# Feed-forward h turned in 32x32 blocks on VectorE and carried between partitions by transfers

## The chip, the cores and the metric

The kernel runs on one core of a Trainium2 chip. Its engines work side by side, each in the order of its own instruction list: TensorE (PE) multiplies matrices, VectorE (DVE) and ScalarE (ACT) work on tiles, GpSimd (POOL) does a little, and SyncE (SP) issues the transfers. Tiles lie in SBUF, 128 partitions wide; TensorE writes into PSUM, which has eight banks. The metric is the device time of one execution in microseconds (us), the median of several runs.

## The reference

Two layers of a streaming encoder on x of 256 x 1024 in float32. Each layer is a feed-forward half step, a mixer (attention over frames and over a memory of 256 entries) and a second feed-forward half step. The change concerns the four feed-forward parts alone:

```python
def swiglu(h, w_gate, w_up, w_down):
    return (jax.nn.silu(h @ w_gate) * (h @ w_up)) @ w_down

for i in range(DEPTH):                                   # DEPTH = 2
    h = rmsnorm(x, ffn1_norm[i])
    x = x + 0.5 * swiglu(h, ffn1_w_gate[i], ffn1_w_up[i], ffn1_w_down[i])
    ...                                                  # the mixer
    h = rmsnorm(x, ffn2_norm[i])
    x = x + 0.5 * swiglu(h, ffn2_w_gate[i], ffn2_w_up[i], ffn2_w_down[i])
```

w_gate and w_up are 1024 x 2816, w_down is 2816 x 1024.

## The kernel before

**Exact products from two parts.** Every operand of a dense product is split into a rounded part and a remainder (hi and lo), and each tile of a product is three matmuls: hi x hi, lo x hi, hi x lo (`dense`, lines 382, 385, 388). The weights are split on the chip.

**The weight stream.** Weights come in 164 chunks of 1 MB, in the order of use. `loader` takes one of three `raw` buffers and issues the chunk's transfers on SP (line 269): for gate and up two of 512 KB, a pair, for down one of 1 MB. `split_hi` casts a chunk in four pieces on ScalarE (line 301, tile hi), `split_lo` subtracts in four pieces on VectorE (line 313, tile lo). There are four buffers of hi and lo. A `raw` buffer is free once lo's fourth piece is done, and only then can the load three chunks later be issued; a hi/lo buffer is free once TensorE has used the chunk.

**A feed-forward part (`ffn`).** The 2816 columns are taken in 11 groups of 256. The gate/up phase makes, for each group, gate and up side by side in one PSUM bank for each of two token blocks (tb 0 and 1; two chunks of weights, 48 matmuls of 512 columns). The down phase then multiplies h by w_down, one chunk of 256 rows for each group, into four banks. Between the two stands `evac`, once a group: for each token block ScalarE makes sil = silu(gate) (line 488) and VectorE multiplies by up (line 491, tile h, tokens on partitions). The down product needs h with its 256 columns on partitions. So TensorE turns it, four 128x128 blocks into one PSUM bank (line 395, tile htp); ScalarE casts that to ht's first part (line 506) and VectorE subtracts for its second (line 508). All 11 ht of a part are kept until the down phase uses them.

**What sets the order.** Nothing is scheduled on the chip: `Flow` (line 47) writes each engine's list beforehand. It keeps its own clock (a matmul 0.216 us, a hop between engines `HOP` 0.22, a 512-wide VectorE operation 0.60) and lets each thread write its next instruction when that clock says that the operands are there. hi and lo pieces are idle threads, placed when their engine is reckoned free within `SLACK` (0.4 us). Threads that are ready go ahead of idle ones. On the chip the lists run in this order, each instruction waiting on semaphores for what it really needs; an instruction that waits holds up all that stand behind it on its engine. In a group the reckoned order on VectorE is: lo's first and second piece of the chunk just freed, h of token block 1, lo's third piece, then (on TensorE) the turns, lo's fourth piece, and with that the next weight pair on SP.

**Transfers and semaphores.** The transfers of the program signal eight semaphores in turn. Before SP issues one, it waits until the transfer eight places earlier has landed.

**Buffers.** SBUF tiles of 4 KB a partition come from `g4` (12 slots), of 2 KB from `g2` (19 slots), PSUM banks from `banks` (8). A thread can wait for slots (`has(n)`).

Of the kernel before, what the change touches and what calls it, by code (L numbers as in the profile page):

```python
# [44 lines left out]


class Flow:
    """Orders the program: work of the vector, scalar and GpSimd engines is placed between the dense
    matrix products by an estimate of when its operands are there."""

    def __init__(self):
        self.now = 0.0
# [90 lines left out]
def kernel(  # L143
# [32 lines left out]
    def bank(name, shape=(P, 4, P)):  # L176
        return banks.take(list(shape), F32, name)

# [1 line left out]
    g1row = const.tile([16, P], F32, name="g1row")  # L180
    nc.sync.dma_start(out=g1row, in_=ffn1_norm.rearrange("l (k p) -> (l k) p", p=P))
    xs = [const.tile([P, D], F32, name=f"x{tb}") for tb in range(2)]
# [52 lines left out]
        nc.vector.tensor_scalar_mul(gcs[:, 3:4], gcol[:, GC_SUB:GC_SUB + 1], 1.0 - LAMBDA_INIT)  # L235
        flow.dve(0, 0.5)

# [1 line left out]
    class Chunk:  # L239
        def __init__(self, parts, mem=False):  # L240
            self.parts, self.mem = parts, mem
# [13 lines left out]
    def add_chunk(parts, uses=8, mem=False):  # L255
        c = Chunk(parts, mem)
        c.uses = uses
        c.index = len(chunks)
        chunks.append(c)
        return c  # L260
# [59 lines left out]
    def k2(t):  # L320
        return t.rearrange("p (k n) -> p k n", k=2)
# [7 lines left out]
    def rows2(w, r):  # L329
        return [(lambda raw: k2(raw), w[r * 256:(r + 1) * 256, :].rearrange("(k p) n -> p k n", p=P))]  # L330

    plan = {}
    WI = (((0, 256), (768, 256)), ((1536, 512),),
          ((256, 256), (1024, 256)), ((512, 256), (1280, 256)), ((2048, 256), (2304, 256)))
# [2 lines left out]
    def plan_ffn(l, nm, wg, wu, wd):  # L337
        gu = []
        for g in range(NG):
            ids = []  # L340
            for c in range(2):
                pieces = 2 if len(chunks) < 2 else 1
                a = cols4(wg[l], c, g * 256, 256, 0, pieces)
                b = cols4(wu[l], c, g * 256, 256, 256, pieces)
                ids.append(add_chunk([q for ab in zip(a, b) for q in ab]))
            gu.append(ids)
        plan[l, nm, "gu"] = gu
        dn = []
        for c in range(NG):
            dn.append(add_chunk(rows2(wd[l], c)))  # L350
            if (l, nm) == (0, 1) and c == NG - 4:
                plan["mem"] = add_chunk(
                    [(lambda raw: raw.rearrange("p (b d) -> p b d", b=2), mem[0].rearrange("(b p) d -> p b d", p=P))],
                    mem=True)
        plan[l, nm, "dn"] = dn
# [17 lines left out]
        plan_ffn(l, 2, ffn2_w_gate, ffn2_w_up, ffn2_w_down)  # L373

    def dense(ps, xh, xl, ready, c, need, sl, start, stop):
        """One K tile of a product: three passes over the parts of both operands."""
        flow.until(lambda: c.lot[need] is not None and ready() is not None)
        flow.at(ready())
        flow.at(c.lot[need])
        at[0] = max(at[0], c.index)  # L380
        wh, wl = sl(c.hi), sl(c.lo)
        nc.tensor.matmul(out=ps, lhsT=xh, rhs=wh, start=start, stop=False)  # L382
        flow.pe(T_MM)
        flow.step()
        nc.tensor.matmul(out=ps, lhsT=xh, rhs=wl, start=False, stop=False)  # L385
        flow.pe(T_MM)
        flow.step()
        nc.tensor.matmul(out=ps, lhsT=xl, rhs=wh, start=False, stop=stop)  # L388
        c.uses -= 1
        if c.uses == 0:  # L390
            hl_left[0] += 1
        return flow.pe(T_MM)

    def turn(dst, src, flipped=False):
        nc.tensor.transpose(out=dst, in_=src, identity=flip if flipped else ident)  # L395
        return flow.pe(T_TR)
# [5 lines left out]
        nc.gpsimd.tensor_tensor(out=dst, in0=v[:, :n], in1=nhalf[:, :n], op=ALU.pow)  # L402
        yield flow.pool(0.3 + 0.165 * n)

# [1 line left out]
    class Xt:  # L406
        def __init__(self):
            self.h = [xtp.tile([P, KT, P], F32R, tag=f"xh{tb}", name=f"xh{tb}") for tb in range(2)]
# [64 lines left out]
            else:  # L473
                yield from prep_half(xt, tb, hf, gc)

# [1 line left out]
    def ffn(l, nm, xt, gc_next):  # L477
        hts = [None] * NG
        htt = [None] * NG

        def evac(g, ps, end):
            hs = []
            for tb in range(2):
                yield lambda: end[tb] is not None and xt.rt[tb] is not None
                yield end[tb]
                yield g2.has(3)
                sil = g2.take([P, 256], F32, "sil")
                nc.scalar.activation(sil, ps[tb][:, 0:256], AF.Silu, scale=xt.r[tb])  # L488
                yield flow.act(256)
                h = g2.take([P, 256], F32, "h")  # L490
                nc.vector.scalar_tensor_tensor(out=h, in0=ps[tb][:, 256:512], scalar=xt.r[tb], in1=sil,  # L491
                                               op0=ALU.mult, op1=ALU.mult)
                t = flow.dve(256, 0.06)
                g2.give()
                banks.give()
                hs.append(h)
            yield t
            yield lambda: banks.left > 0 and g4.left > 0
            tp = bank("htp")
            for f in range(2):  # L500
                for tb in range(2):
                    t = turn(tp[:, 2 * f + tb, :], hs[tb][:, f * P:(f + 1) * P])
            g2.give(2)
            ht = g4.take([P, 2, 4, P], F32R, "ht")
            yield t
            nc.scalar.copy(out=ht[:, 0], in_=tp)  # L506
            yield flow.act(512)
            nc.vector.tensor_sub(ht[:, 1], tp, ht.bitcast(F32)[:, 0])  # L508
            t = flow.dve(512)
            banks.give()  # L510
            hts[g], htt[g] = ht, t

        for g, ids in enumerate(plan[l, nm, "gu"]):
            flow.until(banks.has(2))
            ps = [bank(f"gu{tb}", (P, 512)) for tb in range(2)]
            end = [None, None]
            flow.spawn(evac(g, ps, end))
            order = [(tb, c) for tb in range(2) for c in range(2)] if g == 0 and (l, nm) != (0, 1) else \
                    [(tb, c) for c in range(2) for tb in range(2)]
            for tb, c in order:  # L520
                for k in range(4):
                    kk = 4 * c + k
                    t = dense(ps[tb], xt.h[tb][:, kk, :], xt.l[tb][:, kk, :], lambda: xt.t[tb][kk], ids[c], k,
                              lambda w: k4(w)[:, k, :], kk == 0, kk == KT - 1)
                if c == 1:
                    end[tb] = t
        flow.until(banks.has(4))
        acc = Acc()
        nxt = None if gc_next is None else Xt()
        dn = plan[l, nm, "dn"]  # L530

        def down(c, k, tb, hf):
            sl = slice(hf * 512, (hf + 1) * 512)
            flow.until(lambda: hts[c] is not None)
            ht = hts[c]
            return dense(acc.ps[tb][hf], ht[:, 0, 2 * k + tb, :], ht[:, 1, 2 * k + tb, :], lambda: htt[c], dn[c], 2 * k + hf,
                         lambda w: k2(w)[:, k, sl], c == 0 and k == 0, c == NG - 1 and k == 1)

        SPLIT = NG - 3
        for c in range(SPLIT):  # L540
            for k in range(2):
                for tb in range(2):
                    for hf in range(2):
                        down(c, k, tb, hf)
            g4.give()
            if (l, nm) == (0, 1) and c == SPLIT - 2:
                flow.spawn(memory_prep())
        if nm == 1:
            table_hint(AF.Exp)
        for tb in range(2):  # L550
            flow.spawn(finish(acc, tb, nxt, gc_next, True))
            for hf in range(2):
                for c in range(SPLIT, NG):
                    for k in range(2):
                        t = down(c, k, tb, hf)
                acc.t[tb][hf] = t
        g4.give(NG - SPLIT)
        return nxt
# [2 lines left out]
        nc.scalar.activation(dummy, dummy, func)  # L561
        flow.act(1, 1.3)

# [1 line left out]
    def head_norm(ps, nh, rstd, name):  # L565
        yield g2.has(4)
        sq = g2.take([P, nh * HD], F32, "sq")
# [73 lines left out]
        raw_left[0] += 1  # L641

    def split_evac(dst, src, gain):
        """src (* gain per partition) into its two parts; yields, then returns when both are there."""
        hi, lo = dst
        n = 256
        if gain is None:
            nc.scalar.copy(out=hi, in_=src)
        else:
            nc.scalar.activation(hi, src, AF.Copy, scale=gain)  # L650
        yield flow.act(n)
        if gain is None:
            nc.vector.tensor_sub(lo, src, hi.bitcast(F32))
        else:
            nc.vector.scalar_tensor_tensor(out=lo, in0=src, scalar=gain, in1=hi.bitcast(F32),
                                           op0=ALU.mult, op1=ALU.subtract)
        return flow.dve(n, 0.06)
# [35 lines left out]
            flow.spawn(evac(ps[tb], tb, t))  # L693
        g4.give(4)

# [1 line left out]
    ropeC = const.tile([P, 2, 2, HD], F32, name="ropeC")  # L697
    ropeS = const.tile([P, 2, 2, HD], F32, name="ropeS")
    nlam = const.tile([P, 1], F32, name="nlam")
# [106 lines left out]
                                       op0=ALU.add, op1=ALU.subtract)  # L806
        flow.dve(2)

# [1 line left out]
    def mixer(l, xt, gc_next):  # L810
        typ_a = l % 2 == 0
        bias = {}
# [406 lines left out]
        g4.give(4)  # L1219
        return nxt  # L1220

# [96 lines left out]
```

## Time and profile before

| what | value |
|---|---|
| median of 3 runs | 1004.2 us (1004.04 to 1004.23) |
| span of the profiled execution, first to last instruction | 1001.7 us |
| granted TensorE clock, mean | 1.000 |
| PE idle in the span | 10.6 us |
| matmuls of gate/up (gu), of down (acc from ht) | 2112, 1056 |
| turns of h on PE (htp) | 176, 272 ns each |
| DMA: moved, mean rate | 177.79 MB, 177 GB/s |

The profile has no time of its own for the profiled execution beyond its span; the median of the runs lies 2.5 us above that span. In the rows below, a group of instructions is given by line, engine, operation, out<-in and shape with its count, then total busy time and mean ns of one, then the idle time of the engine just before them and what ended it ("<-PE gu L388" means that the wait ended when that instruction finished). A timeline row begins with start and duration in us. SPq is SP's queue of transfers; the duration there is that of issuing. Matmuls are pipelined: the distance between starts, about 0.23 us, is the pace, not the 0.39 us of one.

### The profile page before, as it was taken

How to read it: one execution, taken by the hardware profiler on the slowest of the kernel's cores; microseconds unless marked ns; L12 is line 12 of the kernel's file. 1: busy time of each engine (PE TensorE's matmuls, PEld its weight loads, DVE VectorE, ACT ScalarE, POOL GpSimd, SP SyncE). 2: the span in 40 equal slices, each digit the busy share in tenths (PEclk: the TensorE clock that was granted, in tenths of full speed). 3: DMA queues.
4: the chain of work that ended last, by engine and by line, in shares of the span. 5: the costliest groups of instructions: out<-in, count | busy, mean ns of one | idle time of the engine just before them, and what ended most of it. 6: DMA issues, size and time to landing. Idle time of an engine off the chain costs nothing.

```text
span 1001.7 us, 13121 instructions
## 1 busy us (share of the span) xinstructions
PE 991.1 (99%) x4772; PEld 817.9 (82%) x4772; DVE 636.3 (64%) x1279; ACT 544.5 (54%) x1159; POOL 58.8 (6%) x65
## 2 busy tenths in 40 slices
PE   8999999999999999999999999999999999999998
PEld 6888888888888888888888888888787888888886
DVE  6756565787666865554466555544989785565542
ACT  6645454776675654554355455444677764554530
POOL 0000000021210000000000000000334100000000
PEclk9999999999999999999999999999999999999999
DMA  8866555575524565655547565555541366655531
GB/s 270 278 189 194 176 202 177 184 253 168 168 85 129 174 202 173 203 171 200 180 126 248 173 203 173 191 188 168 175 162 45 126 210 208 192 186 181 198 126 42
DMA packets 132764, 177.79 MB, mean 177 GB/s; under 512 B 5914, under 2 KB 114011, under 8 KB 132699
## 3 DMA queue, kind: packets, MB, share of 16 engines
q1 hardware_dynamic: 132698, 176.95, 54.9%
q8 instruction: 37, 0.61, 0.2%
q14 instruction: 29, 0.23, 0.1%
HBM read 175.89 MB, written 1.05 MB: 177 GB/s over the span
## 4 chain that ended last, share of the span: by engine, by line
PE 93%; DVE 4%; ACT 1%; DMA 1%; issue 0%; SPq 0%; ACTq 0%
PE gu L382 16%; PE gu L385 16%; PE gu L388 16%; PE acc L385 9%; PE acc L382 9%; PE acc L388 9%; PE pj L388 3%; PE pj L382 2%; PE pj L385 2%; PE htp L395 2%; PE AV L1041 1%; DVE lo L313 1%; PE xtp L395 1%; PE S L973 1%; PE ptp L395 1%; PE kv L388 1%
## 5 line engine op out<-in xcount | busy, mean ns | idle before, releaser
L313 DVE TENSOR_TENSOR lo<-raw,hi 128x512 fp32r<-128x512 f32 x656 | 418.7, 687 | 256.8 <-ACT hi L301 256.5
L301 ACT CAST hi<-raw 128x512 fp32r<-128x512 f32 x656 | 366.0, 618 | 295.6 <-PE gu L388 166.3
L385 PE MATMUL gu<-lo,xh 128*128 128x512 f32 x704 | 277.7, 395 | 0.0
L382 PE MATMUL gu<-hi,xh 128*128 128x512 f32 x704 | 275.0, 391 | 0.0
L388 PE MATMUL gu<-hi,xl 128*128 128x512 f32 x704 | 274.6, 390 | 0.0
L382 PEld LDWEIGHTS gu<-hi,xh 128*128 128x128 f32 x704 | 132.2, 188 | 28.0
L388 PEld LDWEIGHTS gu<-hi,xl 128*128 128x128 f32 x704 | 132.3, 188 | 26.3
L385 PEld LDWEIGHTS gu<-lo,xh 128*128 128x128 f32 x704 | 132.2, 188 | 26.1
L385 PE MATMUL acc<-lo,ht 128*128 128x512 f32 x352 | 137.7, 391 | 0.2 <-DVE lo L313 0.2
L382 PE MATMUL acc<-hi,ht 128*128 128x512 f32 x352 | 137.7, 391 | 0.0
L388 PE MATMUL acc<-hi,ht 128*128 128x512 f32 x352 | 137.5, 391 | 0.0
L385 PEld LDWEIGHTS acc<-lo,ht 128*128 128x128 f32 x352 | 66.1, 188 | 13.9 <-DVE lo L313 0.7
L388 PEld LDWEIGHTS acc<-hi,ht 128*128 128x128 f32 x352 | 66.1, 188 | 13.6
L382 PEld LDWEIGHTS acc<-hi,ht 128*128 128x128 f32 x352 | 66.1, 188 | 13.6
L388 PE MATMUL pj<-hi,xl 128*128 128x512 f32 x160 | 64.4, 403 | 0.0
L385 PE MATMUL pj<-lo,xh 128*128 128x512 f32 x160 | 63.9, 400 | 0.0
L382 PE MATMUL pj<-hi,xh 128*128 128x512 f32 x160 | 63.8, 398 | 0.0
L488 ACT ACTIVATE sil<-gu,xr 128x256 f32<-128x256 f32 x88 | 41.5, 471 | 21.9 <-PE gu L388 21.9
L506 ACT CAST ht<-htp 128x512 fp32r<-128x512 f32 x44 | 25.8, 587 | 37.1 <-PE htp L395 37.1
L491 DVE SCALAR_TENSOR_TENSOR h<-gu,xr,sil 128x256 f32<-128x256 f32 x88 | 42.3, 480 | 2.8
L508 DVE TENSOR_TENSOR ht<-htp,ht 128x512 fp32r<-128x512 f32 x44 | 30.4, 692 | 19.3 <-ACT ht L506 19.3
L402 POOL TENSOR_TENSOR hf<-v,nhalf 128x8 f32<-128x8 f32 (+1 forms) x20 | 30.9, 1546 | 107.3 <-DVE v L400 89.0
(168 smaller groups left out, 835.9 us busy)
## 6 DMA issues: line engine op xcount, KB each, us to landing
raw<-in_ffn_w_down_dram SPq DMA_DIRECT2D x44, 1024.0 KB
raw<-in_ffn_w_gate_dram SPq DMA_DIRECT2D x86, 512.0 KB
raw<-in_ffn_w_up_dram SPq DMA_DIRECT2D x86, 512.0 KB
raw<-in_w_in_dram SPq DMA_DIRECT2D x32, 512.0 KB
raw<-in_w_out_dram SPq DMA_DIRECT2D x8, 1024.0 KB
raw<-in_w_mem_kv_dram SPq DMA_DIRECT2D x4, 1024.0 KB
raw<-in_w_in_dram SPq DMA_DIRECT2D x4, 1024.0 KB
bias<-in_a_rel_bias_dram SPq DMA_DIRECT2D x3, 512.0 KB
```

The lines of the kernel that those rows point to most:

```text
L301: nc.scalar.copy(out=c.hi[:, sl], in_=c.raw[:, sl])
L313: nc.vector.tensor_sub(c.lo[:, sl], c.raw[:, sl], c.hi.bitcast(F32)[:, sl])
L382: nc.tensor.matmul(out=ps, lhsT=xh, rhs=wh, start=start, stop=False)
L385: nc.tensor.matmul(out=ps, lhsT=xh, rhs=wl, start=False, stop=False)
L388: nc.tensor.matmul(out=ps, lhsT=xl, rhs=wh, start=False, stop=stop)
L395: nc.tensor.transpose(out=dst, in_=src, identity=flip if flipped else ident)
L402: nc.gpsimd.tensor_tensor(out=dst, in0=v[:, :n], in1=nhalf[:, :n], op=ALU.pow)
L488: nc.scalar.activation(sil, ps[tb][:, 0:256], AF.Silu, scale=xt.r[tb])
L491: nc.vector.scalar_tensor_tensor(out=h, in0=ps[tb][:, 256:512], scalar=xt.r[tb], in1=sil, op0=ALU.mult, op1=ALU.mult)
L506: nc.scalar.copy(out=ht[:, 0], in_=tp)
L508: nc.vector.tensor_sub(ht[:, 1], tp, ht.bitcast(F32)[:, 0])
L973: nc.tensor.matmul(out=ss[e][:, pr, :nk], lhsT=q[rows, pr, :], rhs=k[rows, pr, :], start=i == 0, stop=i == len(passes) - 1)
```

## The change

- `evac` no longer uses TensorE or a PSUM bank. VectorE writes h with its columns in four blocks of 64 (b), both token blocks in one tile of 4 KB a partition. A VectorE transpose of 128 x 512 transposes each of its 32 x 32 blocks where it stands (tile hb).
- 16 transfers on SP's queue (32 partitions x 512 B each) carry the blocks between the groups of 32 partitions (tile hr): block row a of hb goes to partitions 32b of hr.
- The thread then waits 5.0 us on Flow's clock. The cast and the subtraction that make ht read hr in SBUF, with a rearranged pattern.
- The columns of h now lie on the partitions in another order: partition 32b + i holds columns 64b + i and 64b + 32 + i. `rows_turned` loads w_down to match: four transfers a chunk, each of 256 KB into 32 partitions, in place of one into 128.
- In the down phase the index into ht becomes 2 * tb + k for 2 * k + tb.

Comments and docstrings go too. The core of the diff:

```diff
+    def rows_turned(w, r):
+
+        return [((lambda raw, b=b: k2(raw)[32 * b:32 * b + 32]),
+                 w[r * 256 + 64 * b:r * 256 + 64 * b + 64, :].rearrange("(f i) n -> i f n", f=2)) for b in range(4)]
...
-            dn.append(add_chunk(rows2(wd[l], c)))
+            dn.append(add_chunk(rows_turned(wd[l], c)))
...
         def evac(g, ps, end):
-            hs = []
+            yield g4.has(2)
+            h = g4.take([P, 4, 2, 64], F32, "h")
             for tb in range(2):
...
-                h = g2.take([P, 256], F32, "h")
-                nc.vector.scalar_tensor_tensor(out=h, in0=ps[tb][:, 256:512], scalar=xt.r[tb], in1=sil,
+                nc.vector.scalar_tensor_tensor(out=h[:, :, tb, :],
+                                               in0=ps[tb][:, 256:512].rearrange("p (b j) -> p b j", b=4),
+                                               scalar=xt.r[tb], in1=sil.rearrange("p (b j) -> p b j", b=4),
                                                op0=ALU.mult, op1=ALU.mult)
...
-            yield t
-            yield lambda: banks.left > 0 and g4.left > 0
-            tp = bank("htp")
-            for f in range(2):
-                for tb in range(2):
-                    t = turn(tp[:, 2 * f + tb, :], hs[tb][:, f * P:(f + 1) * P])
-            g2.give(2)
+            yield t
+            yield g2.has(2)
+            hb = g2.take([P, 4, 2, 2, 32], F32, "hb")
+            nc.vector.transpose(out=hb.rearrange("p b t f j -> p (b t f j)"), in_=h.rearrange("p b t x -> p (b t x)"))
+            t = flow.dve(512)
+            g4.give()
+            hr = g2.take([P, 4, 2, 2, 32], F32, "hr")
+            yield t
+            for a in range(4):
+                for b in range(4):
+                    nc.sync.dma_start(out=hr[32 * b:32 * b + 32, a], in_=hb[32 * a:32 * a + 32, b])
+            yield flow.now + 5.0
+            g2.give()
+            yield g4.has()
             ht = g4.take([P, 2, 4, P], F32R, "ht")
-            yield t
-            nc.scalar.copy(out=ht[:, 0], in_=tp)
+            src = hr.rearrange("p a t f j -> p (t f) a j")
+            hi, lo = (ht[:, i].rearrange("p c (a j) -> p c a j", a=4) for i in range(2))
+            nc.scalar.copy(out=hi, in_=src)
             yield flow.act(512)
-            nc.vector.tensor_sub(ht[:, 1], tp, ht.bitcast(F32)[:, 0])
+            nc.vector.tensor_sub(lo, src, hi.bitcast(F32))
             t = flow.dve(512)
-            banks.give()
+            g2.give()
             hts[g], htt[g] = ht, t
...
-            return dense(acc.ps[tb][hf], ht[:, 0, 2 * k + tb, :], ht[:, 1, 2 * k + tb, :], lambda: htt[c], dn[c], 2 * k + hf,
+            return dense(acc.ps[tb][hf], ht[:, 0, 2 * tb + k, :], ht[:, 1, 2 * tb + k, :], lambda: htt[c], dn[c], 2 * k + hf,
```

More of the change, by code (lines that the diff above doesn't have):

```diff
@@ L495, in evac @@
                 banks.give()
-                hs.append(h)
             yield t
-            yield lambda: banks.left > 0 and g4.left > 0
-            tp = bank("htp")
-            for f in range(2):
-                for tb in range(2):
-                    t = turn(tp[:, 2 * f + tb, :], hs[tb][:, f * P:(f + 1) * P])
-            g2.give(2)
+            yield g2.has(2)
[11 more added lines that the diff above has]
+            yield g4.has()
             ht = g4.take([P, 2, 4, P], F32R, "ht")
-            yield t
-            nc.scalar.copy(out=ht[:, 0], in_=tp)
+            src = hr.rearrange("p a t f j -> p (t f) a j")
+            hi, lo = (ht[:, i].rearrange("p c (a j) -> p c a j", a=4) for i in range(2))
+            nc.scalar.copy(out=hi, in_=src)
             yield flow.act(512)
-            nc.vector.tensor_sub(ht[:, 1], tp, ht.bitcast(F32)[:, 0])
+            nc.vector.tensor_sub(lo, src, hi.bitcast(F32))
             t = flow.dve(512)
-            banks.give()
+            g2.give()
             hts[g], htt[g] = ht, t
```

## The prediction

> **What bounds the kernel now.** I read the busy times first, then the chain of waits, then the groups of instructions, then one feed-forward group in the timeline.
>
> ```profile
> span 1001.7 us, 13121 instructions
> PE 991.1 (99%) x4772; PEld 817.9 (82%) x4772; DVE 636.3 (64%) x1279; ACT 544.5 (54%) x1159; POOL 58.8 (6%) x65
> by line: PE gu L382 16.0%; PE gu L385 16.0%; PE gu L388 16.0%; PE acc L385 9.3%; PE acc L382 9.3%; PE acc L388 9.2%; PE pj L388 2.5%; PE pj L382 2.4%; PE pj L385 2.4%; PE htp L395 1.9%; PE AV L1041 1.5%; DVE lo L313 1.3%; PE xtp L395 1.0%;
> ```
>
> TensorE is busy nearly throughout and holds the chain; the turns of h (htp) are 1.9% of it, 19 us. Everything else has slack, so the question is whether what replaces the turns fits into that slack. One group of the feed-forward (the rows are from the timeline; start, duration, engine):
>
> ```profile
> 59.73 0.60 PE L395 MATMUL htp<-ident,h 128*128 128x128 f32 x4
> ...
> 68.34 1.14 ACT L301 CAST hi<-raw 128x512 fp32r<-128x512 f32 x2 [2.24 <-PE gu L388]
> 69.39 0.47 ACT L488 ACTIVATE sil<-gu,xr 128x256 f32<-128x256 f32 x1
> 70.21 0.48 DVE L491 SCALAR_TENSOR_TENSOR h<-gu,xr,sil 128x256 f32<-128x256 f32 x1
> 70.60 1.28 DVE L313 TENSOR_TENSOR lo<-raw,hi 128x512 fp32r<-128x512 f32 x2
> 71.09 0.60 PE L395 MATMUL htp<-ident,h 128*128 128x128 f32 x4
> 71.45 0.48 PE L385 MATMUL gu<-lo,xh 128*128 128x512 f32 x1
> ...
> 71.76 0.40 PE L388 MATMUL gu<-hi,xl 128*128 128x512 f32 x1
> 71.91 0.37 SPq L269 DMA_DIRECT2D raw<-in_ffn_w_gate_dram  x1
> 72.00 0.40 PE L382 MATMUL gu<-hi,xh 128*128 128x512 f32 x1
> 72.33 0.51 SPq L269 DMA_DIRECT2D raw<-in_ffn_w_up_dram  x1
> 72.34 0.69 DVE L508 TENSOR_TENSOR ht<-htp,ht 128x512 fp32r<-128x512 f32 x1 [0.46 <-ACT ht L506]
> ```
>
> A group lasts 71.09 - 59.73 = 11.36 us. hi at 68.34 waited for TensorE to release an operand buffer, not for data: the four buffers are full, and ScalarE fills the one whose use lies three chunks ahead. That lead is what can be lost before TensorE notices.
>
> **What goes.** Four turns delay the next matmul to 71.45 (0.36 us), and that one runs 0.31 to the next where 0.23 to 0.24 is usual: 0.44 us a group, 44 x 0.44 = 19.4 us, which the chain's 19.0 confirms. Without them a group is 10.9 us, a chunk 5.46, and the lead of three chunks 16.4 us. A PSUM bank also goes; nothing waits for one.
>
> **What comes, off TensorE.**
>
> ```profile
> L301 ACT CAST hi<-raw 128x512 fp32r<-128x512 f32 x656 | 366.0, 618 | 295.6 <-PE gu L388 166.3 <-PE acc L388 101.3 <-PE pj L388 10.7
> L506 ACT CAST ht<-htp 128x512 fp32r<-128x512 f32 x44 | 25.8, 587 | 37.1 <-PE htp L395 37.1
> L313 DVE TENSOR_TENSOR lo<-raw,hi 128x512 fp32r<-128x512 f32 x656 | 418.7, 687 | 256.8 <-ACT hi L301 256.5
> L870 DVE TENSOR_TENSOR m<-qkn,ropeC 128x512 f32<-128x512 f32 x6 | 6.5, 1076 | 0.0
> ```
>
> The block turn (128x512 in SBUF) isn't in this trace; between nothing and the 1.08 us of the slowest VectorE row of that size I take lo's 0.69, 44 x 0.69 = 30 us on an engine idle for over 360. The cast of ht reads SBUF: 0.62 for 0.59. Strided operands of h and of ht's subtraction cost 0 to 0.4 us each by the same two rows; I take 0. All this hides unless it is in a loop; such a loop exists, below. The matching row order of the down weights costs nothing in matmuls.
>
> **The transfers.** Each group issues 16 more on SP's queue (16 KB, 32 rows of 512 B), 704 in all. Their prices:
>
> ```profile
> 1.64 0.43 SPq L269 DMA_DIRECT2D raw<-in_ffn_w_gate_dram  x1
> ...
> 3.13 0.47 SPq L269 DMA_DIRECT2D raw<-in_ffn_w_up_dram  x1
> ...
> 18.59 0.37 SPq L269 DMA_DIRECT2D raw<-in_ffn_w_gate_dram  x1
> ...
> 22.01 0.37 SPq L269 DMA_DIRECT2D raw<-in_ffn_w_gate_dram  x1
> 22.42 0.51 SPq L269 DMA_DIRECT2D raw<-in_ffn_w_up_dram  x1
> ...
> 25.20 0.37 SPq L269 DMA_DIRECT2D raw<-in_ffn_w_gate_dram  x1
> 24.97 2.19 ACT L301 CAST hi<-raw 128x512 fp32r<-128x512 f32 x4 [0.93 <-DMA raw<-in_ffn_w_up_dram]
> ...
> 27.94 2.19 ACT L301 CAST hi<-raw 128x512 fp32r<-128x512 f32 x4 [0.30 <-DMA raw<-in_ffn_w_up_dram]
> 0.73 0.40 SPq L181 DMA_DIRECT2D g1row<-in_ffn_norm_dram  x1
> 3.36 0.28 PE L1231 MATMUL gps<-ident,g1row 16*128 16x16 f32 x1
> SPq L269 <- DVE lo L313: 688.7, 139, 18.3
> SPq L269 <- DMA raw<-in_w_mem_kv_dram: 1.6, 1, 1.6
> ```
>
> *Issue*: back to back, 0.41 us (22.01 to 22.42) to 0.50 (four from 1.64 to 3.13, 1.49/3); I take 0.45. *Landing of a weight pair*: 22.01 to 27.94 is 5.9 us, 18.59 to 24.97 is 6.4, since ScalarE there waited for that data; I take 6.3. *Landing of a small one*: g1row's 8 KB had landed 2.6 us after issue (0.73 to 3.36); I take 2.4, between 1.5 (no row has a lower end) and the 3.2 that a slower copy might need. *Completion*: the program gives its transfers eight semaphores in turn, and before each issue SP waits for the one eight places earlier; the last row is such a wait. So at most eight are under way, and with 20 a group every small transfer meets this rule.
>
> By the page "DMA: Bandwidth & Descriptors" of the Trainium skill (section "Rules for kernel authors"), transfers under 64 KB pay mostly overhead, about 2 us each by its section on the anatomy of a DMA; a landing of 2.0 instead of 2.4 would make the forecast below some 18 us less, an estimate; g1row's 2.6 agrees roughly.
>
> **Order on SP.** A weight pair is issued when lo's fourth piece is done (the row with 688.7 us). In the timeline that is 71.88 (70.60 + 1.28), and the pair goes at 71.91. By the program's reckoning the block turn is placed where the turns were, on VectorE between lo's third and fourth piece. The fourth piece, and with it the pair, is written 0.4 us before VectorE is reckoned free of the block turn (SLACK), the small transfers 0.2 us after (HOP): the pair comes ahead by 0.6. Counted from the end of the block turn: lo's fourth piece 0.65, the pair issued at 0.75; six small ones follow, the seventh and eighth wait for the pair itself (semaphores), so the ninth goes no earlier than 0.75 + 6.3 = 7.05; seven more issues, 3.15; landing 2.4: all 16 are there after **12.6 us** (11.1 to 13.9 with the ends above).
>
> **Who waits.** ScalarE's cast of ht needs all 16. The program reckons with 5.0 us from issue to landing and places the cast there, some 9 us behind this group's second sil, where the next group's second sil is 10.8 behind it. ScalarE works in order, so behind the cast stand two hi, that second sil and all later hi; behind them VectorE and finally TensorE. This is a loop: landing, cast of ht (0.59), VectorE's subtraction (0.69), two lo (1.3; the hi and sil run beside), h (0.48), lo's third piece (0.61), block turn (0.65), 4.4 with the hops; then 12.6 until the next landing. It turns once a group in **17.0 us** where TensorE needs 10.9. ScalarE's other work of a group, the rest of its 8 hi, fits into the wait.
>
> **Sum.** ScalarE falls behind by 17.0 - 10.9 = 6.1 us a group, 11 times 67 a feed-forward part; the lead covers 16.4; 51 us of TensorE waiting remain, four times 203. In the down phase no such transfers follow and ScalarE (2.2 us per 5.46) catches up. 1001.7 - 19.4 + 203 = 1185 for the span, and with the 2.5 us by which the median of the runs (1004.2) lies above it **1188 us**. With the ends of the 16 transfers alone, 1122 to 1245.
>
> **The down weights** come in four transfers into 32 partitions each, one issue becoming four: 1.4 us more of SP per 5.46, hidden. Their rate isn't in the trace: pairs of 1 MB follow at 3.2 us (22.01 to 25.20); at half the rate 6.4, above TensorE's 5.46: 0 to 0.9 us on 44 chunks, 0 to 41. I take 0, as anything up to 1.7 times the row is covered. The Trainium skill, page "SBUF — State Buffer", section "Door 1: The DMA port swizzle", speaks against this part: 32 partitions reach half the ports, and its 189 GB/s would be 5.5 us per MB, 4 us in all, an estimate; no run here shows it.
>
> DMA as a whole isn't full (its queue over the span, and 45 us of gate/up):
>
> ```profile
> q1 hardware_dynamic: 132698, 176.95, 54.9%
> 60.00:105.00 45.00, 45.00 (x207) 36.96 (x205) 25.97 (x49) 22.77 (x44) 0.00 (x0) 1.00 0.62 188
> ```
>
> 0.549 x 16 x 1001.7 / 132698 = 66 ns a packet; 512 more a group on 16 engines are 2.1 us of 10.9, 0.19 beside the 0.62 of the gate/up stretch (the window's last number but one).
>
> **Rivals.**
> - *The small transfers go ahead of the pair* (the reckoned times fall otherwise), and their eight predecessors have landed: 15 x 0.45 + 2.4 = 9.2, loop 13.6, 11 x 2.7 - 16.4 = 13, four times 53: 1004.2 - 19.4 + 53 = 1038. Against it: the 0.6 us between the two in the order of writing.
> - *All is hidden, and it is faster*: the loop stays below 10.9 + 16.4/11 = 12.4 us, which needs all 16 landed within 8.0 us. Then 1004.2 - 19.4 = 985. For it: 46% of ScalarE is idle, and 15 x 0.41 + 1.5 = 7.7 would do if nothing stood in front. Against it: the semaphores and the pair. Between these two, near 12.9, gain and loss cancel: 1004.
> - *The down loads bind as well*: up to 41 us on top, 1229.
> - That the change doesn't do what it says: the four turns vanish from the program, so the 19.4 can't stay.
>
> **Chances.** Forecast 56% (1122 to 1245), with the down loads 9%, small ones ahead 16%, all hidden 15%, cancelled 4%. Range 1002 to 1260: it leaves out the hidden case and little above. Faster by over 0.2% (2 us, about what a measurement of this kernel can tell from no change) 0.15, within 0.04, slower 0.81.
>
> **What would show it.** Right: TensorE's idle at lo L313 in the second half of each gate/up phase, ScalarE's cast of ht ended by a DMA wait of some 8 us a group, group period near 17 us once the lead is gone, SP waiting for DMA between the eighth and ninth small transfer. Wrong: the first sil of the next group behind the cast's wait not delaying any hi; SP issuing the 16 within 7 us; a cast of ht late but hi still waiting for PE gu. The number fails if issue costs well under 0.41, if the pair lands sooner than 5.9, or if the lead is larger than three chunks.

## The result and the profile after

The kernel after takes 1267.7 us (median of 4 runs, 1265.5 to 1269.2) against 1004.1 before: the ratio is 1.264, 95% interval 1.2625 to 1.266. The direction is as forecast, 1188 us and the range up to 1260 are not: of a loss of 264 us, 184 were seen coming. The profiled execution spans 1267.3 us. In the runs below, one of the four executions of the kernel without transfers took 3457.5 us where the others took 981.2 to 981.6, and its ratio leaves that one out. The head of its page, the chain of waits and the costliest row of waiting:

```profile
span 1267.3 us, 13934 instructions
PE 1073.2 (85%) x4596; PEld 855.0 (67%) x4596; DVE 651.7 (51%) x1323; ACT 533.0 (42%) x1159; POOL 59.4 (5%) x65
DMA 27%; PE 24%; SPq 22%; DVE 19%; ACT 4%; issue 3%; ACTq 0%
SPq L515 18%; DMA raw<-in_ffn_w_up_dram 10%; DVE lo L313 10%; DMA raw<-in_ffn_w_down_dram 10%; DMA hr<-hb 7%; PE acc L387 3%; PE acc L390 3%; PE acc L393 3%; SPq L269 3%; DVE ht L524 2%; DVE hb L508 2%; ACT ht L522 2%; PE pj L393 2%; PE pj L387 2%; PE pj L390 2%
L522 ACT CAST ht<-hr 128x512 fp32r<-128x512 f32 x44 | 27.2, 618 | 534.9 <-DMA hr<-hb 534.9
```

TensorE held nearly the whole chain before; now it holds 24%, and the largest single entry, 18%, is SP issuing the 16 transfers. ScalarE works 27 us on the 44 casts of ht and waits 535 for their data, 12.2 us each time. That is the wait that the prediction named, half as long again as the 8 us that it gave. TensorE waits behind it; the longest of its waits (us in total, times, longest):

```profile
PE gu L387 <- ACT hi L301: 94.7, 21, 7.2
PE acc L387 <- ACT hi L301: 67.6, 13, 6.4
PE gps L229 <- DMA hr<-hb: 17.0, 1, 17.0
```

The first two are matmuls of gate/up and of down whose hi came late. The third is a wait that the prediction doesn't have; it is taken up below.

What one of the transfers costs on SP is a row of the view of tile hr (duration as least, median and most, in ns):

```profile
L515 SPq DMA_DIRECT2D hr<-hb x704: 507/588/1432, 27.2 to 1225.2; - x176
```

The median is 0.59 us, and in a pass without waits one issue follows the other at 0.62 on average, where the prediction took 0.45. Now one turn of the loop, from one cast of ht to the next (timeline of the kernel after, part 4, without TensorE's rows):

```profile
1099.12 0.62 ACT L522 CAST ht<-hr 128x512 fp32r<-128x512 f32 x1 [11.74 <-DMA hr<-hb]
1099.65 1.13 ACT L301 CAST hi<-raw 128x512 fp32r<-128x512 f32 x2
1099.77 0.69 DVE L524 TENSOR_TENSOR ht<-hr,ht 128x512 fp32r<-128x512 f32 x1 [10.37 <-ACT ht L522]
1100.38 1.29 DVE L313 TENSOR_TENSOR lo<-raw,hi 128x512 fp32r<-128x512 f32 x2
...
1101.59 0.48 DVE L498 SCALAR_TENSOR_TENSOR h<-gu,xr,sil 128x256 f32<-128x256 f32 x1
1101.98 0.68 DVE L313 TENSOR_TENSOR lo<-raw,hi 128x512 fp32r<-128x512 f32 x1
1102.58 0.70 DVE L508 STREAM_TRANSPOSE hb<-h 128x512 f32<-128x512 f32 x1
...
1103.89 0.37 SPq L269 DMA_DIRECT2D raw<-in_ffn_w_gate_dram  x1
...
1104.85 11.02 SPq L515 DMA_DIRECT2D hr<-hb  x16
...
1117.21 0.62 ACT L522 CAST ht<-hr 128x512 fp32r<-128x512 f32 x1 [12.58 <-DMA hr<-hb]
```

Read it downwards. The turn lasts 1117.21 - 1099.12 = 18.09 us. The block turn ends at 1103.28, 4.16 after the cast began (predicted 4.4). The weight pair goes first, as predicted, at 0.61 behind the block turn (predicted 0.75). Then SP issues for 11.02 us: 16 x 0.62 = 9.9, a wait of 0.3 for the pair to land before the eighth, and 0.8 for one issue that took 1.40 where its neighbours took 0.59. The wait between the eighth and the ninth, which the prediction named as a sign, has shrunk to those 0.3 us. The cast starts 1.34 behind the end of the last issue. From the end of the block turn to the data it is 13.93, predicted 12.6.

The starts of the ht casts in the timeline give the mean turn of each feed-forward part: 19.07, 18.27, 18.06 and 18.09 us, where 17.0 was forecast and TensorE needs 10.9.

### The profile page after: what moved, and what is told of

Same layout as the page of the kernel before. It is cut to its first block, busy times and chain, and to the rows that moved or that the text cites. A ratio compares the mean times of both kernels' runs of the same rounds, so it can differ in the third digit from the quotient of the medians.

```text
span 1267.3 us, 13934 instructions
## 1 busy us (share of the span) xinstructions
PE 1073.2 (85%) x4596; PEld 855.0 (67%) x4596; DVE 651.7 (51%) x1323; ACT 533.0 (42%) x1159; POOL 59.4 (5%) x65
## 4 chain that ended last, share of the span: by engine, by line
DMA 27%; PE 24%; SPq 22%; DVE 19%; ACT 4%; issue 3%; ACTq 0%
SPq L515 18%; DMA raw<-in_ffn_w_up_dram 10%; DVE lo L313 10%; DMA raw<-in_ffn_w_down_dram 10%; DMA hr<-hb 7%; PE acc L387 3%; PE acc L390 3%; PE acc L393 3%; SPq L269 3%; DVE ht L524 2%; DVE hb L508 2%; ACT ht L522 2%; PE pj L393 2%; PE pj L387 2%; PE pj L390 2%
## 5 line engine op out<-in xcount | busy, mean ns | idle before, releaser
L387 PE MATMUL gu<-hi,xh 128*128 128x512 f32 x704 | 298.4, 424 | 94.7 <-ACT hi L301 94.7
L390 PE MATMUL gu<-lo,xh 128*128 128x512 f32 x704 | 296.2, 421 | 1.4 <-DVE lo L313 0.9
L393 PE MATMUL gu<-hi,xl 128*128 128x512 f32 x704 | 291.4, 414 | 0.0
L524 DVE TENSOR_TENSOR ht<-hr,ht 128x512 fp32r<-128x512 f32 x44 | 30.5, 692 | 479.0 <-ACT ht L522 479.0
L522 ACT CAST ht<-hr 128x512 fp32r<-128x512 f32 x44 | 27.2, 618 | 534.9 <-DMA hr<-hb 534.9
L387 PEld LDWEIGHTS gu<-hi,xh 128*128 128x128 f32 x704 | 144.2, 205 | 134.6 <-ACT hi L301 103.5
L387 PE MATMUL acc<-hi,ht 128*128 128x512 f32 x352 | 152.6, 434 | 67.6 <-ACT hi L301 67.6
L390 PEld LDWEIGHTS gu<-lo,xh 128*128 128x128 f32 x704 | 144.1, 205 | 42.7 <-DVE lo L313 11.9
L390 PE MATMUL acc<-lo,ht 128*128 128x512 f32 x352 | 151.2, 430 | 0.7 <-DVE lo L313 0.4
L393 PE MATMUL acc<-hi,ht 128*128 128x512 f32 x352 | 148.1, 421 | 0.0
L387 PEld LDWEIGHTS acc<-hi,ht 128*128 128x128 f32 x352 | 73.8, 210 | 88.7 <-ACT hi L301 73.0
L393 PEld LDWEIGHTS acc<-hi,ht 128*128 128x128 f32 x352 | 73.2, 208 | 15.3
```

## The experiments

Ten kernels were run. Each edit is to the kernel after, if not said otherwise; the ratio is to the kernel before, run on the same chip.

| edit | median, us | ratio, 95% interval |
|---|---|---|
| kernel after | 1267.7 | 1.2643, 1.2625 to 1.266 |
| cast of ht 20 us behind the transfers | 1186.7 | 1.1831, 1.1811 to 1.1851 |
| no transfers | 981.5 | 0.9788, 0.9772 to 0.9804 |
| eight transfers of 32 KB | 1047.1 | 1.0444, 1.0428 to 1.0459 |
| eight, cast 20 us behind | 996.6 | 0.9947, 0.9931 to 0.9962 |
| before, down weights in quarters | 1002.4 | 1.0001, 0.9991 to 1.001 |
| transfers read HBM | 1197.8 | one run |
| transfers ahead of the pair | 1222.1 | 1.2173, 1.2123 to 1.2223 |
| on GpSimd's queue, cast 5 us behind | 1236.1 | 1.2316, 1.2292 to 1.2341 |
| on GpSimd's queue, cast 20 us behind | 981.5 | 0.9796, 0.978 to 0.9812 |
| by way of HBM, GpSimd's queue, 20 us | 981.1 | 0.9791, 0.9776 to 0.9805 |

**The cast later.** If ScalarE's in-order wait is all there is, placing the cast where its data is surely there takes the whole loss away.

```diff
-            yield flow.now + 5.0
+            yield flow.now + 20.0
```

> The cast of ht is written 20 us instead of 5 us behind the transfers, so it stands in ScalarE's list behind the work of the next two groups; the 16 transfers stay. Loop theory (ScalarE's list is held up by a cast that waits for the transfers): the loop is gone. What is left is SP's queue: two weight pairs of 0.95 us, 16 transfers at a pace of 0.62 and about 1 us of waiting, 12.8 us a group against TensorE's 10.9; 11 x 1.9 = 21 us a part, against a lead of 16.4 us and some slack of the raw buffers: 985 to 1010 us. Queue theory (the weights behind the transfers come too late, whatever ScalarE does): little changes, above 1200 us.

It took 81 us away and left 184 above the kernel before: neither theory. SP's queue in this run (timeline, SP alone):

```profile
1048.34 0.45 SPq L269 DMA_DIRECT2D raw<-in_ffn_w_gate_dram  x1
1048.83 0.51 SPq L269 DMA_DIRECT2D raw<-in_ffn_w_up_dram  x1
1049.38 12.19 SPq L515 DMA_DIRECT2D hr<-hb  x16
1061.67 0.53 SPq L269 DMA_DIRECT2D raw<-in_ffn_w_gate_dram  x1
1062.24 0.51 SPq L269 DMA_DIRECT2D raw<-in_ffn_w_up_dram  x1
...
1063.89 12.68 SPq L515 DMA_DIRECT2D hr<-hb  x16
...
1092.91 3.99 SPq L269 DMA_DIRECT2D raw<-in_ffn_w_down_dram  x8
1097.02 13.28 SPq L515 DMA_DIRECT2D hr<-hb  x16
```

Each row begins where the one before ends: SP has no gap left. (The passes of 16 are longer than 9.9 us for they hold waits for earlier weight loads to land, 126 us in the whole run.) A group takes 1063.89 - 1049.38 = 14.5 us of it, and 1097.02 + 13.28 - 1092.91 = 17.4 where eight quarter loads for the down phase stand between. TensorE needs a group every 10.9. ScalarE no longer waits for hr but for weights that SP issues too late (the waits of this run; total, times, longest):

```profile
ACT hi L301 <- DMA raw<-in_ffn_w_up_dram: 241.3, 44, 10.2
ACT hi L301 <- DMA raw<-in_ffn_w_down_dram: 219.4, 35, 11.5
```

So there are two limits, and the prediction had worked out only the first: the loop through the cast, 18.1 us a group, and behind it SP's time to issue, with its waits 14.5 to 17.4.

**No transfers.** ht is made from hb; the carrying between partitions is left out, so the down product is computed from h in the wrong places. Everything else stays, the block turn, the strided operands and the quarter loads among it.

```diff
-            for a in range(4):
-                for b in range(4):
-                    nc.sync.dma_start(out=hr[32 * b:32 * b + 32, a], in_=hb[32 * a:32 * a + 32, b])
-            yield flow.now + 5.0
...
-            src = hr.rearrange("p a t f j -> p (t f) a j")
+            src = hb.rearrange("p a t f j -> p (t f) a j")
```

> Leaves out the 16 transfers: ht is made from hb as it stands, so blocks that belong to other partitions are missing. VectorE's block turn, the rearranged casts and the down weights in quarters stay, TensorE's turns are gone. Loop theory: nothing waits for a landing, and only the saving of TensorE is left, 1004 - 19 = 985 us (983 to 988). If the quarters of the down weights or the block turn cost anything on the path, it is above 990; if they are what made the change slow, above 1100.

```profile
PE 969.9 (99%) x4596; PEld 800.4 (82%) x4596; DVE 661.7 (68%) x1323; ACT 545.7 (56%) x1159; POOL 58.8 (6%) x65
```

TensorE is busy for 99% again (the page's head, above), and the time is 20.7 us below that of before. That is what removing the turns is worth. The remaining 286 us of the kernel after, 1267.7 - 981.5, belong to the 16 transfers and to what they hold up.

**Half as many transfers of twice the size.** The same bytes; the blocks land in other places, so the values differ. This tells the price of an issue from that of the bytes.

```diff
-            for a in range(4):
+            for a in range(2):
                 for b in range(4):
-                    nc.sync.dma_start(out=hr[32 * b:32 * b + 32, a], in_=hb[32 * a:32 * a + 32, b])
+                    nc.sync.dma_start(out=hr[32 * b:32 * b + 32, 2 * a:2 * a + 2],
+                                      in_=hb[32 * (3 - b):128 - 32 * b, 2 - 2 * a:4 - 2 * a])
```

> Eight transfers of 32 KB in place of 16 of 16 KB: the same bytes and the same tile filled, but the blocks land in places that aren't those of the transpose. Loop theory with the count of issues as its price: the eighth waits for the weight pair, about 7 us after the block turn, and has landed at 9; the loop is 13.2 us, 11 x 2.3 - 16.4 = 9 us a part, 985 + 36 = 1021 us (985 to 1040). Bytes theory (moving 256 KB within SBUF is what takes the time): unchanged, 1240 to 1270 us.

Its row of tile hr:

```profile
L515 SPq DMA_DIRECT2D hr<-hb x352: 507/588/1639, 26.1 to 1003.7; - x176
```

An issue of 32 KB takes the same 0.588 us as one of 16 KB, and with half of them 221 us of the loss go. The number of transfers counts, not the bytes. 1047 is above the expected range of 985 to 1040: the turn is 13.1 us in part 4, still over 10.9.

**Eight, and the cast later.** The two edits together: 8 issues fit into SP's time, and the cast waits for nothing.

```diff
-            yield flow.now + 5.0
+            yield flow.now + 20.0
```

> Eight transfers of 32 KB in place of 16 of 16 KB (the same bytes; the blocks land in other places, so the products of the down phase are not the reference's), and the cast of ht 20 us behind them. Two-loop theory (two things bind: ScalarE's in-order cast of ht, and the time that SP's queue takes to issue, at about 0.6 to 0.7 us for one transfer from SBUF to SBUF): SP needs 8 x 0.7 + 2 pairs x 0.9 = 7.4 us a group, below TensorE's 10.9, and the cast's wait is gone, so 982 to 990 us, near the 981.5 of the kernel without transfers. Rival, what is left is the bytes or the landing of the blocks: 1020 us or more.

It gave 996.6: neither the expected 982 to 990 nor the rival's 1020. SP's queue (timeline):

```profile
869.51 0.37 SPq L269 DMA_DIRECT2D raw<-in_ffn_w_gate_dram  x1
869.92 0.51 SPq L269 DMA_DIRECT2D raw<-in_ffn_w_up_dram  x1
870.48 5.16 SPq L515 DMA_DIRECT2D hr<-hb  x8
...
880.39 0.37 SPq L269 DMA_DIRECT2D raw<-in_ffn_w_gate_dram  x1
```

In part 4 a group is 880.39 - 869.51 = 10.88 us, TensorE's own pace, and SP has gaps. The 15 us above the kernel without transfers lie in the first part: the casts of ht follow one another there at 12.4 us on average (10.7 without transfers), in the three other parts at 11.2 (10.9 to 11.1). From its first gate/up matmul to its last down matmul the first part takes 200.2 us against 185.5; the other three are the same within 0.1. That part's SP list also carries the loads of the constants, and TensorE waits 3.9 us there for them (gps, as above, which doesn't wait without the transfers); that they are the reason for the rest was not tried alone.

**Down weights in quarters**, built into the kernel before, in the old order of rows.

```diff
-            dn.append(add_chunk(rows2(wd[l], c)))
+            dn.append(add_chunk(rows_quarters(wd[l], c)))
```

> The kernel before, with each chunk of down weights loaded by four transfers into 32 partitions each, in the old row order. Loop theory: the down loads at 4.9 us per MB, as in the profile of the changed kernel, stay below TensorE's 5.46 us a chunk: 1004 us (1001 to 1007). Rival (half the ports hold the down phase up): 1010 us or more, up to 1045.

No difference. One window, of the kernel before and then of this one, a good part of it in the down phase (after the busy times: granted clock, DMA share, GB/s):

```profile
125.00:170.00 45.00, 45.00 (x204) 37.29 (x203) 27.52 (x70) 20.00 (x38) 0.00 (x0) 1.00 0.57 190
```

```profile
125.00:170.00 45.00, 45.00 (x204) 37.27 (x203) 28.07 (x73) 20.52 (x41) 0.00 (x0) 1.00 0.82 188
```

About the same bytes a second keep the DMA engines busy for 0.82 of the time in place of 0.57 (in a second window, from 440 to 500 us, 0.80 for 0.57). It costs nothing while TensorE sets the pace.

**Transfers that read HBM.** The same 16 destinations, but the source is a piece of w_down in HBM; h is not carried, and the transfers don't wait for the block turn.

```diff
-                    nc.sync.dma_start(out=hr[32 * b:32 * b + 32, a], in_=hb[32 * a:32 * a + 32, b])
+                    nc.sync.dma_start(out=hr[32 * b:32 * b + 32, a].rearrange("p t f j -> p (t f j)"),
+                                      in_=(ffn1_w_down, ffn2_w_down)[nm - 1][l, 32 * b:32 * b + 32, a * P:(a + 1) * P])
```

> The kernel after, but each of the 16 transfers reads 32 rows of 512 B of the down weights in HBM in place of hb (h is not what is moved, so the output isn't the reference's, and nothing waits for the block turn). If the source in SBUF is what makes an issue 0.59 us where weight loads take 0.37 to 0.51, the median issue falls to 0.45 us or less, and the time to about 1190 us or less; if the destination of 32 partitions or the number of rows sets it, the median stays at 0.55 to 0.62 us and the time near 1260.

```profile
L515 SPq DMA_DIRECT2D hr<-in_ffn_w_down_dram x704: 310/419/1396, 27.4 to 1154.2; - x176
```

The median issue (view of tile hr) falls to 0.419 us and the time to 1197.8, 70 us less. The pattern written is the same in both traces, 32 rows of 512 B, and in the kernel after SP waited for the block turn only twice (4.7 us in all), so the other source is what is left as the reason; it is one run. Reading SBUF alone doesn't make an issue dear, though: the stores of the result, from SBUF to HBM, are cheap already in the kernel before (four of them, each by itself; view of tile out_dram):

```profile
L472 SPq DMA_DIRECT2D out_dram<-x x4: 333/345/360, 986.5 to 998.8; - x4
```

So the dear ones are the copies with both ends in SBUF (the least of the 704 took 0.507); why was not tried. The weight loads that the prediction took its price from read HBM. With issues at about that price, the turn is 16.4 to 17.2 us, forecast 17.0. That the time is near the 1188 forecast is in part luck: with these turns the prediction's sum gives 1176, 22 less than measured.

**Transfers ahead of the pair.** Written one hop earlier; the later cast only keeps its place in ScalarE's list.

```diff
-            yield t
             for a in range(4):
...
-            yield flow.now + 5.0
+            yield flow.now + 5.9
```

> The kernel after with the 16 transfers written one hop earlier, so that on SP's queue they stand ahead of the weight pair of the same group (the cast 5.9 us behind, in the same place of ScalarE's list). Theory that the pair's place ahead of the transfers costs time: the loop loses the pair's two issues and the waits in the middle of the transfers, 4.2 + 16 x 0.62 + 2.4 = 16.5 us for 18.1; 11 x 1.6 x 4 = 70 us less: about 1197 us (1180 to 1225). Rival, the 16 issues themselves are the price and the order between them and the pair does not matter, since the pair then comes 10 us late: within 20 us of the kernel after, 1248 to 1288.

SP's queue again (timeline):

```profile
1073.76 10.01 SPq L514 DMA_DIRECT2D hr<-hb  x16
1083.87 0.53 SPq L269 DMA_DIRECT2D raw<-in_ffn_w_gate_dram  x1
1084.44 0.51 SPq L269 DMA_DIRECT2D raw<-in_ffn_w_up_dram  x1
...
1089.49 10.01 SPq L514 DMA_DIRECT2D hr<-hb  x16
```

The pass of 16 takes 10.01 us where it took 11.02, the pair's two issues no longer stand in front of it, and the turn is 1089.49 - 1073.76 = 15.7 us here, 16.6 on the mean of part 4. The time fell by 45.6 us to 1222.1, within the range expected of the first theory (1180 to 1225), though above its 1197. So the order on SP costs about 46 us, and the issues themselves remain.

**On GpSimd's queue, cast as in the kernel after.** This separates the two limits from the other side: SP is free, the loop stays.

```diff
-                    nc.sync.dma_start(out=hr[32 * b:32 * b + 32, a], in_=hb[32 * a:32 * a + 32, b])
+                    nc.gpsimd.dma_start(out=hr[32 * b:32 * b + 32, a], in_=hb[32 * a:32 * a + 32, b])
```

> The 16 transfers on GpSimd's queue as in the run at 981.5 us, but the cast of ht placed 5.0 us behind them, as in the kernel after. Two-loop theory: GpSimd does not wait for a weight pair, but the in-order cast still waits for all 16: 4.2 us of work + 16 issues at 0.50 us = 8.0 + semaphore waits of about 1.5 + landing of about 2 give a loop of 15.7 us against TensorE's 10.9; 11 x 4.8 - 16.4 = 36 a part, four times 146, with the 981.5 of the run without transfers about 1125 us (1060 to 1180). Rival, SP's queue alone was the trouble and the place of the cast does not matter: 980 to 990 us.

1236.1, above the whole range of my theory (1060 to 1180), while the rival, SP alone, is refuted by 250 us. GpSimd's timeline in one turn:

```profile
1089.23 1.96 POOL L515 DMA_DIRECT2D hr<-hb  x4 [6.91 <-ACT hi L301]
1093.90 3.90 POOL L515 DMA_DIRECT2D hr<-hb  x8 [2.71 <-issue]
1098.75 1.96 POOL L515 DMA_DIRECT2D hr<-hb  x4 [0.94 <-DMA hr<-hb]
```

The issues are 0.49 us each, 7.8 together, as expected; but from the first to the end of the last pass 1100.71 - 1089.23 = 11.5 us, for 2.71 and 0.94 go in gaps between them, where 1.5 was allowed. The second gap ends with an earlier transfer of the same kind landing; for the first the trace shows no releaser. The turns are 15.5 to 18.3 us in the first six of a part and 18.8 to 21.2 in the last four; why they grow was not looked into. Moving the issues off SP is worth 32 us as long as the cast waits, the slower landing on this queue (4.7 us as the median, from issue) counted in.

**On GpSimd's queue, cast 20 us behind.** Both edits: the transfers of the change, in another queue, and the cast where their data is there.

```diff
-                    nc.sync.dma_start(out=hr[32 * b:32 * b + 32, a], in_=hb[32 * a:32 * a + 32, b])
-            yield flow.now + 5.0
+                    nc.gpsimd.dma_start(out=hr[32 * b:32 * b + 32, a], in_=hb[32 * a:32 * a + 32, b])
+            yield flow.now + 20.0
```

> The 16 transfers are issued on GpSimd's queue and the cast of ht stands 20 us behind them. Two-loop theory: SP's queue holds the weights alone, as before; if one issue takes GpSimd up to 0.65 us, 16 are 10.4 us a group, below 10.9, and the time is 982 to 995 us. If one issue takes about 1 us, 16 us a group on GpSimd bind in place of SP, and with 20 us of delay for the cast: 1050 to 1100 us. Rival, the number of small transfers binds wherever they are issued (landing, DMA engines): 1150 us or more, as with the cast late alone (1186.7).

981.5 us, the time of the kernel without transfers: all 704 are hidden. Rows of its tile hr, and of its waits:

```profile
L515 POOL DMA_DIRECT2D hr<-hb x704: 496/496/667, 25.1 to 935.0; - x176
DMA to landing us min/median/max: 1.6/4.5/8.6
```

```profile
ACT hi L301 <- PE gu L393: 180.4, 81, 2.9
ACT ht L522 <- DMA hr<-hb: 20.6, 8, 5.5
```

The cast still waits for hr now and then (20.6 us in all), but ScalarE waits mostly for TensorE to release buffers, the mark of a full lead. In the section "Issuing engine by pattern" of the page "DMA: Bandwidth & Descriptors", the Trainium skill gives simple copies to SP and calls SP's path generally the faster. Here an issue on GpSimd takes 0.50 us against SP's 0.59, and only the landing is slower there (4.5 us as the median from issue; on SP 1.9 in the turn quoted, 1.34 + 0.59). For these copies, once they have time to land, the idle queue is the better one.

**By way of HBM.** One store of hb (256 KB) to a tile in HBM and four loads of 64 KB from it, on GpSimd's queue, cast 20 us behind: 5 issues for 16.

```diff
+            dr = dramp.tile([P, 512], F32, tag="dr", name="dr")
+            nc.gpsimd.dma_start(out=dr, in_=hb.rearrange("p b t f j -> p (b t f j)"))
+            dv = dr.rearrange("(a i) (b x) -> b i a x", a=4, b=4)
+            for b in range(4):
+                nc.gpsimd.dma_start(out=hr[32 * b:32 * b + 32].rearrange("p a t f j -> p a (t f j)"), in_=dv[b])
+            yield flow.now + 20.0
```

> In place of the 16 transfers one store of hb to a tile in HBM (256 KB) and four loads from there into 32 partitions each (64 KB), five issues on GpSimd's queue, the cast of ht 20 us behind. Two-loop theory: five issues bind no queue and two landings one after the other are over before the cast: 980 to 992 us, faster than both kernels. Rival, bytes through the DMA engines bind (twice as many here as with the 16): 1100 us or more.

981.1 us: twice the bytes cost nothing either. This and the run before it cannot be told apart (0.9791 and 0.9796); both beat the kernel before by about 2%.

## Why the prediction was wrong in size

**Held: the mechanism.** The cast of ht, placed 5.0 us behind its transfers, stops ScalarE; its hi come late, and TensorE waits. The cast's 535 us of waiting fit it, and two pairs of runs show it: the cast later is worth 81 us on SP's queue and 1236.1 - 981.5 = 255 us on GpSimd's. The order on SP (pair first) and the loop's work of 4.16 us (predicted 4.4) were right too.

**Held: the saving and the parts taken as free.** The four turns were put at 19.4 us; the kernel without transfers is 20.7 faster. So the block turn, the strided operands (the subtraction takes 0.69 us in both kernels, h 0.48) and the quarter loads together cost nothing on the end. The block turn's own row in the view of tile hb, against the 0.69 taken from lo:

```profile
L508 DVE STREAM_TRANSPOSE hb<-h x44: 702/705/707, 25.5 to 1211.5; 128x512 f32<-128x512 f32 x44
```

The rate of the quarter loads, which the trace before could not show, can now be seen after the last ht of part 4, where ScalarE waits for each down chunk (ScalarE's timeline, kernel after):

```profile
1233.21 2.19 ACT L301 CAST hi<-raw 128x512 fp32r<-128x512 f32 x4 [1.42 <-DVE lo L313]
1238.12 2.18 ACT L301 CAST hi<-raw 128x512 fp32r<-128x512 f32 x4 [2.72 <-DMA raw<-in_ffn_w_down_dram]
1243.03 2.18 ACT L301 CAST hi<-raw 128x512 fp32r<-128x512 f32 x4 [2.72 <-DMA raw<-in_ffn_w_down_dram]
1247.82 2.18 ACT L301 CAST hi<-raw 128x512 fp32r<-128x512 f32 x4 [2.61 <-DMA raw<-in_ffn_w_down_dram]
```

Three chunks in 14.61 us are 4.9 us per MB, or less if something else held them: 1.5 times the 3.2 of the row used, within the 1.7 that the prediction gave as cover, and below TensorE's 5.46. The rule of the Trainium skill ("SBUF — State Buffer", "Door 1: The DMA port swizzle") that spoke against this part made it 5.5, an estimate: its direction agrees, its size is a little too slow.

**Failed: "I take 0.45" for an issue.** This is the term that was mis-sized. The rows behind it, 0.37 to 0.51, are all of loads from HBM; the new transfers read SBUF, where an issue measures 0.59. No row before showed a copy within SBUF (the stores of the result leave it), so the price should have been left open upwards, and the range with it; instead the own ends of the forecast went from 0.41 to 0.50. With HBM as the source the issue is 0.42 and the kernel takes 1198. In the turn the error is 13.93 for 12.6 us and not more, for a second term was too large: the wait of the seventh and eighth transfer for the pair (6.3 us, taken as exposed) passes beside the dearer issues of those before them, and 0.3 us of it are left. The landing was 1.9 where 2.4 was taken. (The 2 us or so that the prediction quotes from the Trainium skill, page "DMA: Bandwidth & Descriptors", section "Anatomy of one DMA — SWDGE (gpsimd) path", are given there for transfers issued on GpSimd; on that queue the median here was 4.5.)

**What the longer turn explains.** The prediction's own sum with the measured turns: they exceed 10.9 by 8.17, 7.37, 7.16 and 7.19 us; 11 x 29.89 = 329, less four times the lead of 16.4 is 263, less 19.4 for the turns removed 244. The spans differ by 1267.3 - 1001.7 = 266. So the formula accounts for 244, where it gave 184 with 17.0. The other 22 are open in part. By the matmuls' times the four parts are longer by 79.1, 61.8, 64.9 and 60.5 us and the stretches between them are the same within 0.2, so the sum is short by 10.5, 2.0, 7.4 and 2.7.

In part 1 TensorE waits once for 17.0 us (gps above), to turn the gains that come in by small loads, one behind each weight pair on SP; the last of these is issued at 102.2 us where it was 72.9 before, and the turn runs at 107.0. The profile puts the wait down to a transfer hr<-hb, which signals the same eight semaphores as those loads. In the kernel before, and without the transfers, the trace has no such wait. How much of the 10.5 it makes was not tried alone, nor whether the lead was full when the parts began, nor what the lower granted clock (below) does.

**Where TensorE waits.** The prediction expected the waits behind lo in the second half of gate/up, and ScalarE catching up in the down phase, where "no such transfers follow". Nearly all of them end with hi (1.3 us with lo), and the casts of the last groups run on into the down phase: of the 266 us, 157 come in the gate/up phases and 109 in the down phases. And that TensorE's idle time is 194 us, near the 203 forecast, is luck: 17 of it are that one wait, and the matmuls, slower by 103 us in all (1073 us busy against 970 without the transfers), presumably fill a part of what would have been waiting.

**Not seen: SP's queue is a limit of its own.** The prediction counted SP's issues only inside the loop and found the rest hidden. 16 x 0.62, the waits among them and two pairs are 14.5 us a group in the late-cast run, over TensorE's 10.9, whatever ScalarE does. So the rival "all is hidden" was further off than written: it named a landing within 8.0 us as its condition, and the late cast, which gave every landing its time, still left 1187. At the 0.45 taken, 16 x 0.45 and two pairs at 0.9 are 9.0 us without waits, under 10.9: the same mis-sized price hid the second limit.

**The rival of the small transfers first** (1038) fell with the same price: its turn was put at 13.6 and measured 16.6, and the time 1222. The rival of the down loads as a limit (1229) is refuted by the quarter loads alone at 1002.4. What remained of the rival "hidden, 985" came true on the other queue.

## What to carry to other kernels

Many small transfers are priced first by their count times the issue time of exactly that kind of copy, as a load on the issuing queue over the period that it must keep; a row of a copy between other memories is no bound for it. Then look for what stands behind the first consumer in its engine's order, and place that consumer no earlier than issue, semaphore waits and landing together allow. With 16 transfers both had to be mended here, late consumer and idle queue: the first alone gave 81 us of the 286, the second alone 32, and both together all of it.

## What was not expected of the hardware

- An issue on SP cost here by the memories at its ends and not by its size: 0.588 us (median) from SBUF to SBUF and 0.419 from HBM to SBUF, for the same 16 KB into the same 32 partitions, and 0.33 to 0.36 for the four stores from SBUF to HBM. Twice the size left the first at 0.588.
- TensorE's granted clock was lower the more it had to wait: 1.000 on the mean in the kernel before and in the one without transfers (99% busy), 0.985 with eight transfers (95%), 0.937 with the late cast (88%) and 0.907 in the kernel after (85%). In a stretch of part 1 with many waits it was 0.82 (a window; the granted clock is the third number from the end):

```profile
60.00:180.00 120.00, 82.30 (x316) 64.64 (x315) 48.56 (x90) 37.61 (x76) 0.00 (x0) 0.82 0.49 140
```

82.30 busy us for 316 matmuls are 0.26 us each, against 0.22 in the kernel before (45.00 for 204, in the window above). So the busy share of 85% on the page overstates how much TensorE gets done.
